# Experts by halves of the gate/up columns, token gather by fp32 matmuls for two experts at a time, a ring of 22 weight pieces

## The chip, the cores and the metric

One core of a Trainium2 chip runs one program. The metric is device time in microseconds (us) of one execution; lower is better.

## What is computed

One layer: a mixer of three branches over 256 tokens of width 1024, then a mixture of 32 experts of which each token takes 4, then a norm. All weights are fp32. The part that matters here is the expert stage and the few lines ahead of it:

```python
logits = (x @ w_router + b_router)                 # 256 tokens, 32 experts
top_logit, top_idx = lax.top_k(logits, 4)
top_w = jax.nn.softmax(top_logit, axis=-1)
...
xb = x[tok]                                        # the tokens of expert e
gu = xb @ w_gu[e] + b_gu[e]                        # 1024 x 2048
gate, up = jnp.split(gu, 2, axis=-1)
gate = jnp.minimum(gate, 7.0); up = jnp.clip(up, -7.0, 7.0)
act = (up + 1) * gate * jax.nn.sigmoid(1.702 * gate)
y[tok] += weight * (act @ w_down[e] + b_down[e])   # 1024 x 1024
...
out = rmsnorm(x + gate_ffn * y, norm_final)
```

## The kernel before, in words

The mixer and its projections take the first two fifths of the program. After them come the output projection (four column blocks `pr`, line 904 on), which builds the residual `x1` block by block and at once feeds the router matmuls (`lps`, line 933), then the router (lines 945 to 981), and then a loop over the 32 experts (line 1224).

An expert's weights are 12 pieces of 1 MiB, 128 rows of 8 KB: eight pieces of `w_gu`, one for each block of 128 input rows and with all 2048 gate and up columns, and four of `w_down`. `ew` (line 848) issues one DMA for a piece on the SP queue into the next tile of a ring. The ring has `NR = (8, 7, 4)`, 19 tiles, in three pools that are opened as the mixer's memory falls free. A load waits until the matmuls have read its tile's last piece, and the loads stand in one queue, so the ring decides how far the loads run ahead of the matmuls. The first loads are issued during the last mixer stages (`ew_ahead`).

At most 64 tokens are taken per expert. `gather` (lines 1005 to 1028) picks them by matmul with a one-hot matrix `oh`: `x1` times its row scale `rs2` is split into two fp32r parts `xshi` and `xslo` (lines 983 to 986, two on ACT and two on DVE of 128x1024), and four experts' tokens are gathered at once into `xe`, of which there are two buffers. An expert then runs

- `gate_up` (line 1046): for each of 8 row blocks `k` the gate tile `pg` and the up tile `pu`, each by two matmuls that fill partitions 0 to 63 and 64 to 127;
- `scatter` of the expert before (line 1087), the transposes for the way back (`swt_ps`), the bias matmul of the next expert's gate tile;
- `act_half` (line 1055) for columns of half `c`: min, sigmoid, products on DVE and ACT, transposes on PE (`act_ps`), copy on ACT; then `down_half`, four of eight row blocks of `w_down`; and both again for the second half.

The Tile framework's scheduler sets the order of the instructions on each engine and of the loads on SP from priorities (`issue_after` moves a block behind an instruction). At expert 29 `gain` (line 1107) broadcasts the final norm's gain by four matmuls on diagonal matrices that DVE builds. The last expert is finished by `down_finish` (line 1118): its down result in two column blocks of 256, the residual by matmuls with the identity (`ylast`), squares, root, and `norm` with the four output DMAs.

Each matmul of fp32 operands shows as two instructions in the trace, each transpose and each fp32r matmul as one.

Of the kernel before, what the change touches and what calls it, by code (L numbers as in the profile page):

```python
# [18 lines left out]
D = 1024  # L19
# [5 lines left out]
GRP = 4  # L25
# [55 lines left out]
def trace(tc, pools, I, out, dbg, stop):  # L81
# [746 lines left out]
    NR = (8, 7, 4)  # L828
    nload, lastew = [0], [None]

    DN_ORDER = (0, 1, 4, 5, 2, 3, 6, 7)
    gsrc = I["w_gu"].rearrange("e (q k p) n -> e q p k n", p=128, k=1)
    dsrc = I["w_down"].rearrange("e q p (k n) -> e q p k n", k=2)
# [14 lines left out]
    def ew(src):  # L848
        t = ew_tile()
        lastew[0] = SY.dma_start(t.rearrange("p (k n) -> p k n", k=src.shape[1]), src)  # L850
        return t

    epieces = iter([gsrc[e, q] if q < 8 else dsrc[e, DN_ORDER[2 * (q - 8)] // 2] for e in range(NE) for q in range(12)])
    ahead = []

    def ew_ahead(n):

        with tc.issue_after(last[0].ins):
            for _ in range(n):
                ahead.append(ew(next(epieces)))  # L860

    def ew_next():
        return ahead.pop(0) if ahead else ew(next(epieces))
# [5 lines left out]
    for br, (yhl, pw) in enumerate(((ybhl, "p_sb"), (yahl, "p_lru"), (None, "p_rwkv"))):  # L869
# [6 lines left out]
        for pr in range(4):  # L876
# [3 lines left out]
            if br == 2 and pr == KS:  # L880
                gmix = mt("gmix", [128, 512])
                row_bcast(adag[:, 0:4], gmix)
                keep_setup(mixer)
                bias_setup(mixer)
# [19 lines left out]
    for pr in range(4):  # L904
# [15 lines left out]
        if pr == 2:  # L920
            gmix = mt("gmix", [128, 512])
            row_bcast(adag[:, 4:8], gmix)
        for t in range(2):
            V.tensor_tensor(ps[:, t], ps[:, t], gmix[:, pr % 2 * 256:pr % 2 * 256 + 256], ALU.mult)
            V.tensor_tensor(x1[:, t, csl], x1[:, t, csl], ps[:, t], ALU.add)
            A.activation(ps[:, t], x1[:, t, csl], AF.Square, accum_out=sqp[:, t, pr:pr + 1])
# [4 lines left out]
            V.tensor_copy(xt, tp)  # L931
# [6 lines left out]
    pools.close(wsp, fin)  # L938
    moe2 = pools("moe2", bufs=1, side="right")
# [27 lines left out]
    for t in range(2):  # L967
        A.activation(wd[:, t], lg[:, t], AF.Exp, bias=sm[:, t, 0:1])
        A.activation(sm[:, t, 4:8], sm[:, t, 4:8], AF.Exp, bias=sm[:, t, 0:1], accum_out=sm[:, t, 1:2])
    V.reciprocal(sm[:, :, 1:2], sm[:, :, 1:2])  # L970
    for t in range(2):
        V.scalar_tensor_tensor(wd[:, t], wd[:, t], sm[:, t, 1:2], sel[:, t], ALU.mult, ALU.mult)
    dump("lg", lg)

    cps = ptp([128, NE], "cnt_ps")
    for t in range(2):
        T.matmul(cps[0:1], onesq[:, 0:1], sel[:, t], start=(t == 0), stop=(t == 1))
    cnt = mt("cnt", [1, 1])
    V.tensor_reduce(cnt, cps[0:1], AX.X, ALU.max)
    cnt_i = moe.tile([1, 1], I32, name="cnt_i")  # L980
    V.tensor_copy(cnt_i, cnt)

    xs = [mt2(n, [128, 2, D], dt=F32R) for n in ("xshi", "xslo")]
    for t in range(2):
# [20 lines left out]
    def gather_start(rks, n):  # L1005

        oh = mt2("oh", [128, 2, GRP, SLOTS], dt=F32R)
        for t in range(2):
            V.tensor_tensor(oh[:, t, 0:n], bcast(iot[:, 0:SLOTS], 1, n), bcast(rks[t], 2, SLOTS), ALU.is_equal)
        return oh, mt2("xe", [128, KT, GRP, SLOTS], 2)  # L1010

    def gather_part(oh, xe, n, ks):

        for k in ks:
            xps = ptp([128, 2, GRP, SLOTS], "xps")
            for kk in range(2):
                for t in range(2):
                    for i, x in enumerate(xs):
                        T.matmul(xps[:, kk, 0:n].rearrange("p e s -> p (e s)"), x[:, t, (k + kk) * 128:(k + kk + 1) * 128],  # L1019
                                 oh[:, t, 0:n].rearrange("p e s -> p (e s)"), start=(kk + t + i == 0), stop=(t + i == 2),  # L1020
                                 skip_group_check=True)
# [21 lines left out]
    def pgu_tile(name):  # L1043
        return psum.tile([128, 512], F32, name=name, tag="mm", bufs=3)

    def gate_up(pg, pu, gu, xe):
        for k in range(KT):
            for j, p in enumerate((pg, pu)):
                for hf in range(2):
                    c0 = j * D + hf * 512  # L1050
                    i = T.matmul(p[hf * 64:hf * 64 + 64], xe[:, k], gu[k][:, c0:c0 + 512], start=False, stop=(k == KT - 1),  # L1051
                                 skip_group_check=True)
        return i

    def act_half(c, pg, pu, ahead=False):

        csl = slice(c * 256, c * 256 + 256)
        g_, s_ = (mt2(n, [128, 256], b) for n, b in (("g_", 2), ("s_", 1)))
        V.tensor_scalar(g_, pg[:, csl], 7.0, None, ALU.min)
        A.activation(s_, g_, AF.Sigmoid, scale=1.702)  # L1060
        if ahead:
            sqrt_ahead(s_)
        V.tensor_tensor(g_, g_, s_, ALU.mult)
        V.tensor_scalar(s_, pu[:, csl], 7.0, -7.0, ALU.min, ALU.max)
        V.scalar_tensor_tensor(g_, s_, 1.0, g_, ALU.add, ALU.mult)
        tp = ptp([128, 2, 128], "act_ps")
# [5 lines left out]

    def down_half(pd, dn, c, at):
        for n in range(c * 4, c * 4 + 4):
            k = DN_ORDER[n]
            w = dn[n // 2][:, k % 2 * D:k % 2 * D + D]
            for hf in range(2):
                i = T.matmul(pd[hf * 64:hf * 64 + 64], at[:, k % 2, (k // 4) * 64:(k // 4) * 64 + 64],  # L1078
                             w[:, hf * 512:hf * 512 + 512], start=(n == 0), stop=(n == KT - 1))
# [7 lines left out]
    def scatter(yd, swt):  # L1087

        for t in range(2):
            for hf in range(2):  # L1090
# [4 lines left out]
                V.tensor_tensor(y[:, t, csl], y[:, t, csl], ps, ALU.add)  # L1095

    def expert(gu, dn, bias, xe, swt):
        pg, pu = pgu_tile("pg"), pgu_tile("pu")
        bias(0, pg)
        bias(1, pu)  # L1100
        gate_up(pg, pu, gu, xe)
        pd = pch([128, 512], "pd")
        for c in range(2):
            down_half(pd, dn, c, act_half(c, pg, pu))
        scatter(gated(pd), swt)

    def gain(t):

        for i in range(0, KT, 2):
            ps = pch([128, 256], "gfin")  # L1110
            T.matmul(ps, onesq, diag2(mt("gdiag", [128, 2, 128], 1, "s_w"), P("norm_final", i, 2)), start=True, stop=True)
            A.activation(t[:, i * 128:i * 128 + 256], ps, AF.Copy)
        return t

    PRE, LATE = 6, 4
    odst = out.rearrange("b (a p) d -> p (b a) d", p=128)

    def down_finish(ats, dn, swt, gfin):
# [3 lines left out]
        pds = [pch([128, 256], "pd") for _ in range(2)]  # L1122

        lastmm = [None]

        def down(n):
            k = DN_ORDER[n]
            w = dn[n // 2][:, k % 2 * D:k % 2 * D + D]
            for j in range(2):
                for hf in range(2):  # L1130
                    lastmm[0] = T.matmul(pds[j][hf * 64:hf * 64 + 64], ats[k % 4 // 2][:, k % 2, (k // 4) * 64:(k // 4) * 64 + 64],
                             w[:, hf * 512 + j * 256:hf * 512 + j * 256 + 256], start=(n == 0), stop=(n == KT - 1))

        for n in range(PRE):
            down(n)
        ys = [pmm("ylast") if i < 3 else pch([128, 512], "ylast") for i in range(4)]
        for i in range(4):
            with tc.issue_after(lastmm[0].ins) if i >= LATE else contextlib.nullcontext():
                T.matmul(ys[i], ident, y[:, i // 2, i % 2 * 512:i % 2 * 512 + 512], start=True, stop=False, skip_group_check=True)
# [197 lines left out]
```

## Time and profile before

| | us |
|---|---|
| runs shown: median of 3 | 1546.18 |
| lowest and highest of them | 1539.46, 1547.42 |
| the profiled execution, its own time | 1557.08 |
| its span (what the trace covers) | 1555.3 |
| PE busy in the span | 1458.0 (94%) |
| DVE, ACT, POOL busy | 638.5, 411.5, 11.0 |
| first and last expert load issued | 520.7, 1515.0 |
| mean granted TensorE clock | 0.969 of full |

Times inside the trace are counted from the span's start. Matmuls are pipelined and their ends are modelled: the pace of a row of matmuls is read from the starts, not from the length of one. "DMA" is the share of the 16 DMA engines that was busy. A granted clock of 1.00 is 2.4 GHz, of 0.50 is 1.2 GHz.

### The profile page before, as it was taken

To read this page: it belongs to the slowest core of one execution; us is meant where nothing else is said; L and a number is where in the kernel's file an instruction comes from. 1 tells how busy PE (TensorE), PEld (TensorE's weight loads), DVE (VectorE), ACT (ScalarE), POOL (GpSimd) and SP (SyncE) were. 2 spreads that over 40 slices of the span, in tenths; PEclk is the share of its full clock that TensorE was granted. 3 is DMA by queue.
4 is the path that set the end of the run, shared out by engine and by line. 5 is a ranking of instruction groups with operands and counts; after the bars stand their busy time and mean duration, and the time that the engine had idled before them with its cause. 6 is when DMAs were issued, how large, how long until landed. Compare 5 with 4: busy or idle time off the path is not lost. (4 is left out here: it accounts for less than half of the span.)

```text
span 1555.3 us, 21129 instructions
## 1 busy us (share of the span) xinstructions
PE 1458.0 (94%) x8592; PEld 834.1 (54%) x8592; DVE 638.5 (41%) x1322; ACT 411.5 (26%) x728; POOL 11.0 (1%) x59
## 2 busy tenths in 40 slices
PE   6999999999899998999999999999989989989897
PEld 4888989788899896333333333333223323323233
DVE  4677536689735664213223133123113113212313
ACT  4654335668534443001001001001001001001101
POOL 0000000000000000000000000000000000000000
PEclk8999889999899998999999999999999999999999
DMA  9455345346333876999999999999999999999994
GB/s 374 156 182 184 126 134 187 108 143 217 99 95 125 312 296 267 367 421 422 421 421 421 421 421 421 421 420 421 422 422 421 421 422 421 421 421 422 421 421 190
DMA packets 85686, 498.87 MB, mean 321 GB/s; under 512 B 12624, under 2 KB 12880, under 8 KB 36432
## 3 DMA queue, kind: packets, MB, share of 16 engines
q1 hardware_dynamic: 85584, 497.46, 80.4%
q8 instruction: 70, 1.15, 0.3%
q14 instruction: 32, 0.26, 0.0%
HBM read 496.37 MB, written 1.05 MB: 320 GB/s over the span
## 5 line engine op out<-in xcount | busy, mean ns | idle before, releaser
L1051 PE MATMUL pg<-ew,xe 128*64 128x512 f32 x1024 | 274.6, 600 | 20.5 <-DMA ew<-in_w_gu_dram 20.3
L1051 PE MATMUL pu<-ew,xe 128*64 128x512 f32 x1024 | 267.8, 593 | 0.0
L1078 PE MATMUL pd<-ew,act 128*64 128x512 f32 x992 | 233.0, 606 | 27.6 <-ACT act L1070 27.6
L168 PE MATMUL mm<-hhi,whi 128*128 128x256 f32 x656 | 193.2, 295 | 3.9 <-ACT gq L723 2.9
L168 PE MATMUL mm<-hhi,wlo 128*128 128x256 f32 x656 | 192.7, 294 | 3.4 <-DVE wlo L150 3.4
L168 PE MATMUL mm<-hlo,whi 128*128 128x256 f32 x656 | 191.3, 292 | 0.0
L150 DVE TENSOR_TENSOR wlo<-raw,whi 128x1024 fp32r<-128x1024 f32 x122 | 148.7, 1221 | 80.9 <-ACT whi L149 79.9
L1051 PEld LDWEIGHTS pg<-ew,xe 128*64 128x64 f32 x1024 | 70.6, 137 | 171.6 <-issue 103.6
L149 ACT ACTIVATE whi<-raw 128x1024 fp32r<-128x1024 f32 x122 | 128.6, 1057 | 123.1 <-PE mm L168 77.0
L1051 PEld LDWEIGHTS pu<-ew,xe 128*64 128x64 f32 x1024 | 76.4, 137 | 142.9 <-issue 140.4
L1078 PEld LDWEIGHTS pd<-ew,act 128*64 128x64 f32 x992 | 70.0, 138 | 153.9 <-issue 111.1
L168 PEld LDWEIGHTS mm<-hhi,whi 128*128 128x128 f32 x656 | 129.1, 197 | 12.3 <-issue 5.6
L168 PEld LDWEIGHTS mm<-hhi,wlo 128*128 128x128 f32 x656 | 128.9, 196 | 10.0 <-issue 5.1
L168 PEld LDWEIGHTS mm<-hlo,whi 128*128 128x128 f32 x656 | 129.1, 197 | 5.3 <-issue 4.8
L1084 DVE TENSOR_TENSOR yd<-pd,gff 128x512 f32<-128x512 f32 x31 | 21.5, 692 | 244.8 <-PE pd L1078 226.0
L1093 PE MATMUL pc<-yd,swt 64*128 64x512 f32 x248 | 96.0, 628 | 0.0
L1095 DVE TENSOR_TENSOR x<-x,pc 128x512 f32<-128x512 f32 x124 | 84.1, 681 | 9.3 <-PE pc L1093 8.3
L1093 PEld LDWEIGHTS pc<-yd,swt 64*128 64x128 f32 x248 | 30.0, 185 | 49.7 <-issue 29.9
L1023 ACT ACTIVATE xe<-xps,adaf,A 128x256 f32<-128x256 f32 x32 | 18.1, 564 | 96.2 <-DVE xe L1022 95.9
L1070 ACT ACTIVATE act<-act_ps 128x256 f32<-128x256 f32 x64 | 24.5, 383 | 59.9 <-PE act_ps L1068 58.8
L206 PE MATMUL adaps<-raw,crep 128*32 128x256 f32 x384 | 31.6, 433 | 7.9 <-DMA raw<-in_w_ada_dram 7.8
L1022 DVE TENSOR_SCALAR xe<-xps,A,adaf 128x256 f32<-128x256 f32 x32 | 17.4, 544 | 45.4 <-PE xps L1019 45.4
(814 smaller groups left out, 1769.2 us busy)
## 6 DMA issues: line engine op xcount, KB each, us to landing
ew<-in_w_gu_dram SPq DMA_DIRECT2D x256, 1024.0 KB, 19.8
ew<-in_w_down_dram SPq DMA_DIRECT2D x128, 1024.0 KB, 19.8
raw<-in_w_in_dram SPq DMA_DIRECT2D x90, 512.0 KB, 3.7
raw<-in_w_ada_dram SPq DMA_DIRECT2D x48, 512.0 KB, 4.5
raw<-in_p_sb_dram SPq DMA_DIRECT2D x8, 512.0 KB, 4.1
raw<-in_p_lru_dram SPq DMA_DIRECT2D x8, 512.0 KB, 3.4
raw<-in_p_rwkv_dram SPq DMA_DIRECT2D x8, 512.0 KB, 7.5
raw<-in_w_out_dram SPq DMA_DIRECT2D x8, 512.0 KB, 4.6
```

Source lines behind the costliest of these rows:

```text
L149: A.activation(hi, src, AF.Copy)
L150: V.tensor_tensor(lo, src, r32(hi), ALU.subtract)
L168: T.matmul(ps[:, c], w[i][:, k, c * 128:c * 128 + 128], x[j][:, q * 4 + k], start=(q + c + k + n == 0), stop=(q == 1 and k == 3 and n == 2 ...
L206: T.matmul(ps[32 * j:32 * j + 32], crep[:, q * 4 + j, :], raw[q][:, j], start=(q == 0), stop=(q == 1))
L1022: V.tensor_scalar(xe[:, k, 0:n], xps[:, 0, 0:n], A2[:, k:k + 1], sh2[:, k:k + 1], ALU.mult, ALU.add)
L1023: A.activation(xe[:, k + 1, 0:n], xps[:, 1, 0:n], AF.Identity, scale=A2[:, k + 1:k + 2], bias=sh2[:, k + 1:k + 2])
L1051: i = T.matmul(p[hf * 64:hf * 64 + 64], xe[:, k], gu[k][:, c0:c0 + 512], start=False, stop=(k == KT - 1), skip_group_check=True)
L1070: A.activation(at, tp, AF.Copy)
L1078: i = T.matmul(pd[hf * 64:hf * 64 + 64], at[:, k % 2, (k // 4) * 64:(k // 4) * 64 + 64], w[:, hf * 512:hf * 512 + 512], start=(n == 0), st ...
L1084: V.tensor_tensor(yd, pd, gff2, ALU.mult)
L1093: T.matmul(ps, swt[sl, t], yd[sl], start=True, stop=True)
L1095: V.tensor_tensor(y[:, t, csl], y[:, t, csl], ps, ALU.add)
```

## The change

- `w_gu` is laid out on the host as eight pieces of another cut: four pieces for gate and up columns of half 0 (each 256 + 256 columns of either partition half, two row blocks), then four for half 1. `gate_up` runs one half into one PSUM tile `pgu`; its activations (`act_chain`) follow at once, and the transposes (`act_back`) stand behind the other half's matmuls. The biases are laid out to match.
- The split into `xshi` and `xslo` goes. `oh` holds `rs2` at the hits instead of 1, and the gather multiplies fp32 `x1` by it: for two experts (`GRP = 2`) at a time, so 16 times in place of 8, into one `xe` buffer. `y` becomes a tile of its own, since `x1` stays in use.
- A fourth ring pool of 3 tiles is opened where `wsp` and `fin` close, so the ring has 22 tiles. `gmix` moves into `wsp`.
- In the output projection the squares go to a PSUM tile of their own, and the copies `x1t` go from DVE to ACT. The softmax weights and the count (`weights`) are traced behind the first one-hots.
- `gain` becomes one DMA that broadcasts `norm_final` into a ring tile, issued behind the last expert's loads.
- Last expert: the last piece is loaded as two halves; `w_down` pieces are cut so that column quarters `j` lie together; the second down blocks run for `j = 0`, then `j = 1`, each followed by its gating, scatter, squares and product with the gain; `end_norm` scales.

```diff
-GRP = 4
+GRP = 2
-    NR = (8, 7, 4)
+    NR = (8, 7, 4, 3)
...
-    epieces = iter([gsrc[e, q] if q < 8 else dsrc[e, DN_ORDER[2 * (q - 8)] // 2] for e in range(NE) for q in range(12)])
+    epieces = iter([(gsrc[e, q] if q < 8 else dsrc[e, q - 8], 2 if e == NE - 1 and q == 11 else 1)
+                    for e in range(NE) for q in range(12)])
...
-            A.activation(ps[:, t], x1[:, t, csl], AF.Square, accum_out=sqp[:, t, pr:pr + 1])
+            A.activation(pch([128, 256], "sqj"), x1[:, t, csl], AF.Square, accum_out=sqp[:, t, pr:pr + 1])
...
-            V.tensor_copy(xt, tp)
+            A.activation(xt, tp, AF.Copy)
...
     pools.close(wsp, fin)
+    ring_open()
+    ew_ahead(NR[3])
...
-    xs = [mt2(n, [128, 2, D], dt=F32R) for n in ("xshi", "xslo")]
-    for t in range(2):
-        A.activation(xs[0][:, t], x1[:, t], AF.Copy, scale=rs2[:, t:t + 1])
-        V.scalar_tensor_tensor(xs[1][:, t], x1[:, t], rs2[:, t:t + 1], r32(xs[0][:, t]), ALU.mult, ALU.subtract)
-    y = x1
+    y = mt2("y", [128, 2, D])
...
-        oh = mt2("oh", [128, 2, GRP, SLOTS], dt=F32R)
-        for t in range(2):
-            V.tensor_tensor(oh[:, t, 0:n], bcast(iot[:, 0:SLOTS], 1, n), bcast(rks[t], 2, SLOTS), ALU.is_equal)
-        return oh, mt2("xe", [128, KT, GRP, SLOTS], 2)
+        oh = mt2("oh", [128, 2, GRP, SLOTS])
+        for e in range(n):
+            for t in range(2):
+                V.tensor_scalar(oh[:, t, e], iot[:, 0:SLOTS], rks[t][:, e:e + 1], rs2[:, t:t + 1], ALU.is_equal, ALU.mult)
+        return oh, mt2("xe", [128, KT, GRP, SLOTS])
...
-                    for i, x in enumerate(xs):
-                        T.matmul(xps[:, kk, 0:n].rearrange("p e s -> p (e s)"), x[:, t, (k + kk) * 128:(k + kk + 1) * 128],
+                    T.matmul(xps[:, kk, 0:n].rearrange("p e s -> p (e s)"), x1[:, t, (k + kk) * 128:(k + kk + 1) * 128],
...
+    def gate_up(p, c, gu, xe, ks=range(KT)):
+        for k in ks:
+            w = gu[c * 4 + k // 2].rearrange("p (k h n) -> p k h n", k=2, h=2)[:, k % 2]
+            for hf in range(2):
+                i = T.matmul(p[hf * 64:hf * 64 + 64], xe[:, k], w[:, hf], start=False, stop=(k == KT - 1),
+                             skip_group_check=True)
...
+        for j in range(2):
+            js = slice(j * 256, j * 256 + 256)
+            for n in (6, 7):
+                for hf in range(2):
+                    down_mm(pds[j], dn, n, at, hf, slice(j, j + 1))
             V.tensor_tensor(yd[:, js], pds[j], gff2[:, js], ALU.mult)
...
+                    A.activation(ptp([128, 256], "junk"), p, AF.Square, accum_out=ss[:, t, j * 2 + hf:j * 2 + hf + 1])
+                    V.tensor_tensor(o_[:, t, n:n + 256], p, gfin[:, n:n + 256], ALU.mult)
...
-    xe, swt = gather(*ranks_of(0)), back_of(0)
+    oh, xe = gather_start(*ranks_of(0))
+    weights()
+    gather_part(oh, xe, GRP, range(0, KT, 2))
...
-        i = gate_up(pg, pu, gu, xe[:, :, e % GRP])
+        i = gate_up(p0, 0, gu, x)
+        g0 = act_chain(p0)
         with tc.issue_after(i.ins):
             if held:
-                scatter(*held)
+                scatter(*held, first=(e == 1))
...
+            i = gate_up(p1, 1, gu, x)
...
+        g1 = act_chain(p1, end)
+        with tc.issue_after(i.ins):
+            at = act_back(g0)
```

Where it moves instructions. DVE in the router, before: `lg` are the scaled logits, `m_6530` the four greatest, `sel` the chosen experts, `rk` a token's place in its expert.

```order
L956 MEMSET m_6530 128x2x4
L986 SCALAR_TENSOR_TENSOR xslo<-x_4491,rs_6522,xshi 128x1024
L958 MATCH_REPLACE sel<-m_6530,lg 128x32 x2
L986 SCALAR_TENSOR_TENSOR xslo<-x_4491,rs_6522,xshi 128x1024
L959 TENSOR_TENSOR sel<-sel,lg 128x64
```

The same place now:

```order
L960 MEMSET m_6547 128x2x4
L962 MATCH_REPLACE sel<-m_6547,lg 128x32 x2
L963 TENSOR_TENSOR sel<-sel,lg 128x64
L977 RECIPROCAL sm<-sm 128x2
L979 SCALAR_TENSOR_TENSOR wd<-wd,sm,sel 128x32 x2
L970 TENSOR_TENSOR rk<-tp,sel 128x32
```

The two `xslo` stood between the logits and `sel`; nothing stands there now.

PE in an expert late in the loop (from the matmuls of its first pieces to its last down matmul), before; the `pg` and `pu` pair stands eight times in all ahead of these rows:

```order
L1093 MATMUL pc<-yd,swt 128x512 x3
L1037 MATMUL swt_ps<-ident,s_w 128x128 x2
L1213 MATMUL pg<-bgt,pick 128x512
L1093 MATMUL pc<-yd,swt 128x512
L1068 MATMUL act_ps<-ident,g__9432 128x128 x2
L1078 MATMUL pd<-ew,act 64x512 x8
```

The same stretch now, of an expert behind which a gather stands:

```order
L1055 MATMUL pgu<-ew,xe 64x512 x16
L1103 MATMUL pc<-yd,swt 128x512 x3
L1055 MATMUL pgu<-ew,xe 64x512 x4
L1103 MATMUL pc<-yd,swt 128x512
L1055 MATMUL pgu<-ew,xe 64x512 x12
L1075 MATMUL act_ps<-ident,g__10745 128x128 x2
L1041 MATMUL swt_ps<-ident,s_w 128x128 x2
L1210 MATMUL pgu<-bgt,pick 128x512
L1083 MATMUL pd<-ew,act 64x512 x8
L1023 MATMUL xps<-oh,x_4491 128x128 x8
```

The scatter stands inside the second half's matmuls, and the first half's transposes stand directly behind them.

PE at the first expert, now. `ew_5158` and `ew_5286` are the first and second piece of half 0, `ew_5692` the first piece of half 1.

```order
L1055 MATMUL pgu_6625<-ew_5158,xe_6573 64x512 x2
L1055 MATMUL pgu_6627<-ew_5692,xe_6573 64x512 x2
L1023 MATMUL xps_6601<-oh_6568,x1_4491 128x128 x4
L1055 MATMUL pgu_6625<-ew_5158,xe_6573 64x512 x2
L1055 MATMUL pgu_6627<-ew_5692,xe_6573 64x512
L1055 MATMUL pgu_6625<-ew_5286,xe_6573 64x512
L1023 MATMUL xps_6608<-oh_6568,x1_4491 128x128 x4
L1055 MATMUL pgu_6625<-ew_5286,xe_6573 64x512 x3
```

Here both halves run side by side between groups of four gather matmuls; eight gather matmuls stand ahead of these rows. The first piece falls free behind the fourth row, the second behind the last.

## Rows read from the trace of the kernel before

**Rows 1.** The page, part 2: GB/s moved in 40 equal slices of the span.
```profile
GB/s 374 156 182 184 126 134 187 108 143 217 99 95 125 312 296 267 367 421 422 421 421 421 421 421 421 421 420 421 422 422 421 421 422 421 421 421 422 421 421 190
```

**Rows 2.** The page, part 6: issues of a line, KB each, median us to landing.
```profile
ew<-in_w_gu_dram SPq DMA_DIRECT2D x256, 1024.0 KB, 19.8
```

**Rows 3.** Windows: length, busy per engine (count), then PE clock, DMA share, GB/s.
```profile
600.00:605.00 5.00, 1.05 (x7) 0.97 (x7) 4.10 (x17) 4.53 (x9) 0.00 (x0) 0.63 0.37 156
605.00:610.00 5.00, 4.90 (x26) 4.46 (x28) 2.47 (x11) 0.56 (x1) 0.00 (x0) 0.50 0.01 3
610.00:615.00 5.00, 5.00 (x22) 2.08 (x24) 1.09 (x2) 1.13 (x2) 0.00 (x0) 0.85 0.23 66
...
635.00:640.00 5.00, 5.00 (x22) 2.23 (x20) 0.85 (x2) 0.80 (x2) 0.00 (x0) 1.00 0.35 146
```

**Rows 4.** Timeline of the SP queue: start, length, issue, count.
```profile
574.97 12.75 SPq L850 DMA_DIRECT2D ew<-in_w_gu_dram  x7
...
612.67 0.33 SPq L850 DMA_DIRECT2D ew<-in_w_gu_dram  x1
...
639.34 5.38 SPq L850 DMA_DIRECT2D ew<-in_w_gu_dram  x5
```

**Rows 5.** Timeline of the router: start, length, engine, line, operation.
```profile
601.30 1.27 DVE L986 SCALAR_TENSOR_TENSOR xslo<-x,rs,xshi 128x1024 fp32r<-128x1024 f32 x1
...
602.81 1.28 DVE L986 SCALAR_TENSOR_TENSOR xslo<-x,rs,xshi 128x1024 fp32r<-128x1024 f32 x1
...
604.00 0.22 DVE L959 TENSOR_TENSOR sel<-sel,lg 128x64 f32<-128x64 f32 x1
...
606.23 0.55 PE L1019 MATMUL xps<-oh,xshi 128*128 128x256 f32 x1
...
609.91 1.86 PE L1051 MATMUL pg<-ew,xe 128*64 128x512 f32 x4
```

**Rows 6.** Timeline of PE, an expert that waits for no load.
```profile
1184.71 1.08 PE L1051 MATMUL pg<-ew,xe 128*64 128x512 f32 x4
...
1198.60 1.98 PE L1093 MATMUL pc<-yd,swt 64*128 64x512 f32 x6
...
1202.16 0.44 PE L1068 MATMUL act_ps<-ident,g__9432 128*128 128x128 f32 x2
1203.14 3.66 PE L1078 MATMUL pd<-ew,act 128*64 128x512 f32 x16 [0.53 <-ACT act L1070]
...
1207.97 3.65 PE L1078 MATMUL pd<-ew,act 128*64 128x512 f32 x16 [0.53 <-ACT act L1070]
1211.46 1.03 PE L1051 MATMUL pg<-ew,xe 128*64 128x512 f32 x4
```

**Rows 7.** Timeline of PE: half a gather, first and last; fp32 matmuls of 128 columns.
```profile
1182.60 0.39 PE L1019 MATMUL xps<-oh,xshi 128*128 128x256 f32 x1
...
1184.50 0.28 PE L1019 MATMUL xps<-oh,xslo 128*128 128x256 f32 x1
...
190.79 1.16 PE L533 MATMUL nps<-sav,bk 128*128 128x128 f32 x8
```

**Rows 8.** Timeline of PE: a wait for a load, in brackets, late in the loop.
```profile
1222.49 1.08 PE L1051 MATMUL pg<-ew,xe 128*64 128x512 f32 x4 [0.54 <-DMA ew<-in_w_gu_dram]
```

**Rows 9.** Timeline of PE and a window, around the broadcast of the norm's gain.
```profile
1478.78 5.19 PE L1078 MATMUL pd<-ew,act 128*64 128x512 f32 x16 [0.32 <-ACT act L1070]
...
1472.00:1476.00 4.00, 2.73 (x5) 1.32 (x6) 0.94 (x3) 0.77 (x2) 0.00 (x0) 0.50 1.01 420
```

**Rows 10.** A window and the timeline of PE at the end of the program.
```profile
1530.00:1535.00 5.00, 5.00 (x19) 2.24 (x20) 3.31 (x8) 2.67 (x5) 0.00 (x0) 1.00 0.39 164
...
1527.28 1.03 PE L1051 MATMUL pu<-ew,xe 128*64 128x512 f32 x4
...
1534.41 5.40 PE L1131 MATMUL pd<-ew,act 128*64 128x256 f32 x48
...
1540.79 1.95 PE L1131 MATMUL pd<-ew,act 128*64 128x256 f32 x16
```

More of the change, by code (lines that the diff above doesn't have):

```diff
@@ L859, in ew_ahead @@
             for _ in range(n):
-                ahead.append(ew(next(epieces)))
+                ahead.append(ew(*next(epieces)))
     def ew_next():
-        return ahead.pop(0) if ahead else ew(next(epieces))
+        return ahead.pop(0) if ahead else ew(*next(epieces))
     mhl, KS = None, 1
@@ L1094, in scatter @@
                 csl = slice(hf * 512, hf * 512 + 512)
-                V.tensor_tensor(y[:, t, csl], y[:, t, csl], ps, ALU.add)
+                V.tensor_tensor(y[:, t, csl], (x1 if first else y)[:, t, csl], ps, ALU.add)
     def expert(gu, dn, bias, xe, swt):
[L1098 to L1101, printed above, removed]
+        ats = []
+        for c in range(2):
+            p = pgu_tile()
+            bias(c, p)
+            gate_up(p, c, gu, xe)
+            ats.append(act_back(act_chain(p)))
@@ L1102, in expert, with gain @@
         pd = pch([128, 512], "pd")
         for c in range(2):
-            down_half(pd, dn, c, act_half(c, pg, pu))
+            down_half(pd, dn, c, ats[c])
         scatter(gated(pd), swt)
[L1107 to L1112, printed above, removed]
+    def gain():
+        t = ew_tile()[:, 0:D]
+        SY.dma_start(t, I["norm_final"][0].partition_broadcast(128))
@@ L1120, in down_finish @@
+    def down_finish(pds, dn, at, swt, gfin):
         o_ = ew_tile().rearrange("p (t d) -> p t d", t=2)
         ss = mt("ss2", [128, 2, 8], 1, "m8")
[L1122 to L1128, printed above, removed]
+        for n in (4, 5):
             for j in range(2):
                 for hf in range(2):
-                    lastmm[0] = T.matmul(pds[j][hf * 64:hf * 64 + 64], ats[k % 4 // 2][:, k % 2, (k // 4) * 64:(k // 4) * 64 + 64],
-                             w[:, hf * 512 + j * 256:hf * 512 + j * 256 + 256], start=(n == 0), stop=(n == KT - 1))
@@ L1134, in down_finish @@
[L1134 to L1139, printed above, removed]
-        for n in range(PRE, KT):
-            down(n)
+                    i = down_mm(pds[j], dn, n, at, hf, slice(j, j + 1))
@@ L1144, in down_finish @@
             js = slice(j * 256, j * 256 + 256)
+            for n in (6, 7):
+                for hf in range(2):
+                    down_mm(pds[j], dn, n, at, hf, slice(j, j + 1))
             V.tensor_tensor(yd[:, js], pds[j], gff2[:, js], ALU.mult)
@@ L1284, in trace @@
             gu = [ew(gsrc[bass.ds(e, 1), q][0]) for q in range(8)]
[L1285 removed]
+            dn = [ew(dsrc[bass.ds(e, 1), q][0]) for q in range(4)]
             for b in range(1, S // SLOTS):
```

194 lines of the change are left out of this document (103 added, 91 removed).

## Prediction

> **What bounds the kernel now.** I read the page's bandwidth line first, then windows of five us where that line changes, then the SP queue and PE around the gaps. The line sits at 421 GB/s from the eighteenth slice to the last but one [rows 1]: the expert stage moves weights as fast as they come. A piece of 1 MiB takes 1.048576 MB / 421 GB/s = 2.49 us, the twelve of an expert 29.9 us. A load lands 19.8 us after its issue [rows 2], eight pieces of 2.49, so the queue is eight deep and the matmuls wait for it, not it for them: late in the loop PE stops half a us for a piece [rows 8], while an expert that waits for nothing takes 1211.46 - 1184.71 = 26.75 us [rows 6].
>
> So two things set the end. One is **when the queue runs without a gap**. The loads fill 19 tiles and stop near 602: the DMA share falls from 0.37 to 0.01 [rows 3], and the next load is issued at 612.67, when the first expert's first piece has been read [rows 4]. A second hole stands before 640 (0.35): the 28th load waits until 639.34. From there the loads run through. The other is **what comes after the last landing**. The engines fall quiet at 1530 + 0.39 x 5 = 1531.95 [rows 10], the span ends at 1555.3, 23.35 us later. In that tail PE is behind: it reads the last piece until 1540.79 + 1.95 = 1542.74, 10.8 us after it landed. Part of that lag was made earlier: building the norm's gain stalled PE and the granted clock was 0.50, 1.2 GHz, in 1472 to 1476, where sixteen down instructions took 5.19 us for 3.65 at full clock [rows 6, 9].
>
> **The first gap.** The router's chain runs on DVE: `sel` at 604.00, first gather matmul at 606.23, first expert matmul at 609.91 [rows 5]. Both `xslo` (1.27 and 1.28 us) stood ahead of `sel` and go: `sel` at 601.45. The `x1t` copies leave DVE too, and the square no longer holds the PSUM tile that DVE multiplies; I take 0.8 us for both, so 600.6. Against it, the softmax weights now stand ahead of `rk` on DVE; I take 0.6 us (below 0.4, above 1.5, the table load and exponents of ACT late by that much). First gather matmul: 600.6 + 2.23 + 0.6 = 603.4.
>
> An fp32 matmul of 128 columns is two instructions; eight such instructions took 1.16 us, of which the last one's modelled end is some 0.3: 0.112 each [rows 7]. The sixteen ahead of the first expert take 1.8 us at full clock, 3.6 at half, which is what this place had (0.50, [rows 3]). The first expert matmul then stands at 605.2 to 607.0; I take 606. The bounds are 604.8, and 609.9 if nothing of this is on the path.
>
> A matmul of `gate_up` costs 13.89 / 32 = 0.434 us [rows 6], a detour of four gather matmuls 0.9 + 0.3. By the new order the first piece is free after six matmuls and one detour, 3.8 us, the second after eight more steps' worth (two matmuls, a detour, three matmuls), 3.4 us: 606 + 7.2 + 0.5 for a clock still low = 613.7. Meanwhile the three new tiles keep the DMA busy 7.5 us longer, to about 609.4; their pool opens when the last output-projection products are read, before 599, so I cost that wait at nothing. What follows, in the order of the releases, is one piece per 1.7 us at most times, faster than 2.49, and the hole before 640 closes: the load that now needs the first down piece is the 35th, not the 28th.
>
> So: before, 27 pieces had landed at 639.34 + 0.8 (from issue to flow) = 640.1. After, 23 have landed at 613.7 + 0.8 = 614.5. The last landing moves by 640.1 - 614.5 - 4 x 2.49 = **15.6 us** earlier. With the bounds of the first matmul it is 10.5 to 17.
>
> **The loop.** PE's own time per expert changes, and DMA covers it as long as it stays under 29.9. The wait of 0.98 us from `act_ps` to the first down matmul [rows 6] is now filled by `swt_ps` and the bias matmul that stood elsewhere: 26.75 - 0.75 = 26.0. The gather: half of one took 1184.50 - 1182.60 + 0.2 = 2.1 us for four experts [rows 7], so about 4.2 us per four. Now 32 instructions per two experts, 32 x 0.112 = 3.6 us plus switches and waits for PSUM, 4.4: 2.2 us per expert instead of 1.05. Together **28.2 us**, 1.7 under DMA. I cost it at nothing, but its cover is thin. At 640 the queue would be 23 + 25.5 / 2.49 = 33 pieces on, PE about 17, so PE has some 37 us to make up, and about 8 for the expert that adds the down biases, in 29 experts at 1.7, 49 us. It arrives with about 4 us to spare. Moving four activations of a half behind matmuls, DVE's 64-column one-hots and the smaller evacuations are off the path: DVE is busy 41% of the span.
>
> **The tail**, counted from the last landing. The last gate/up piece lands 4 x 2.49 = 9.95 us before it; four matmuls, 1.7, end at -8.2. One identity matmul 0.9, transposes and copy 1.0, the first down piece 1.8 (sixteen instructions at 5.40 / 48 = 0.112, [rows 10]), two identity matmuls 1.7, transposes 1.0, two pieces 3.6, one identity matmul 0.9, the last piece 1.8: +4.4 instead of +10.8, **6.4 us**. The lag that the norm's gain made is gone with it: that becomes one DMA behind the last weights. From the last down matmul to the end were 12.6 us; gating, squares and products of the first columns now run beside the second's, for which I take 1.0. Tail: **7.4 us**, between 0 if PE is late and 9.
>
> **The sum.** 15.6 + 7.4 = 23.0 us off the profiled execution, 1557.08 to 1534.1. That execution stood 10.9 us above the median of the runs shown, which itself lies in a spread of 8 us. Off the median: 1546.18 - 23.0 = **1523**.
>
> **Rivals.**
> - **PE does not catch up.** If an expert costs PE 28.6 instead of 28.2, the 4 us to spare become 29 x 0.4 - 4 = 8 late at the last expert, and the tail's gain is gone: 1531. For it: the cover is thin and PSUM tiles for the gather are shared with the transposes. Against it: the early experts' order leaves PE fewer gaps than the stretch of rows 6. 0.20.
> - **The three tiles fill late.** If the new pool waits for something past 609, 7.5 us go: 1531. Against it: nothing in its releasers runs that late. 0.06.
> - **Slower: the fp32 gather makes PE the bound.** Place: the 32 instructions between two experts. At 0.224 us each, the half-clock price, a pair's gather costs 8 us, an expert 30, PE never catches up, and ends some 48 us behind: 1571. It decides from 0.17 us per instruction, where an expert is 29.1 us and the lag eats all 23. Against it: 0.112 [rows 7]. 0.06.
> - **The clock falls in the waits.** When PE has caught up it waits 1.7 us per expert. In this trace waits of 0.54 us stand between matmuls at the full-clock 0.27 us each [rows 8], and the long one beside the gain stands with 0.50 [rows 9]. Should each of the last seven experts lose its clock for 11 us, each would lose 5.5 - 1.7 = 3.8 us, 27 in all: 1550. [...] 0.03.
>
> **Chances and range.** Forecast 0.63, rivals as given, 0.02 for the rest. A measurement of this kernel can tell some 0.5%, 7.7 us, from no change. Faster by more holds the forecast and nearly all of the first two rivals, 0.88; within it 0.05; slower 0.07. The forecast's own bounds are 16 to 26 us, 1520 to 1530; with the spread of the runs, 4 us to either side, and the first rival, 1513 to 1537.
>
> **What would show it.** Right: no xslo; `sel` near 601 and the first expert matmul near 606; the DMA share without a hole after 615 and none before 609; last landing 13 to 17 us earlier in the span; PE waits for loads again in the last experts; under 19 us from the last landing to the end. Wrong: gather instructions further apart than 0.15 us, an expert above 28.5 us, no waits for loads at the end, a granted clock under 1.00 late in the loop, or a hole in the DMA share near 640.

## Result and the profile after

Ten executions of the change took 1528.99 to 1540.28 us, median **1534.23**; ten of the kernel before 1539.46 to 1555.27, median 1546.80. The ratio is 0.992, 95% interval 0.9903 to 0.9937: 12.6 us faster, about 10 to 15. Forecast were 23 us and 1523, range 1513 to 1537. The sign, the side of 0.5% and the range hold; the size came out at little more than half. Two of the timed executions of the experiments below (1912.0 us in the kernel with the earlier way back, 1802.0 in the one with two stalls) ran at mean granted clocks of 0.73 and 0.74 and are left out of every median and ratio.

The page's bandwidth row, as [rows 1], reaches the ceiling one slice earlier, in the seventeenth instead of the eighteenth:

```profile
GB/s 378 159 183 184 163 153 170 110 166 182 91 97 120 279 301 371 423 420 422 421 421 421 421 422 421 421 421 421 421 421 421 421 421 421 422 420 421 421 421 229
```

The windows that answer to [rows 3] (length, busy per engine, then PE clock, DMA share, GB/s):

```profile
600.00:605.00 5.00, 5.00 (x29) 3.50 (x28) 0.82 (x2) 0.92 (x2) 0.00 (x0) 0.83 1.02 419
605.00:610.00 5.00, 5.00 (x24) 2.21 (x25) 1.34 (x5) 0.92 (x2) 0.00 (x0) 1.00 0.60 203
610.00:615.00 5.00, 5.00 (x24) 1.60 (x23) 0.97 (x4) 1.67 (x2) 0.00 (x0) 1.00 0.68 246
...
635.00:640.00 5.00, 5.00 (x26) 1.71 (x24) 0.00 (x0) 0.00 (x0) 0.00 (x0) 1.00 1.02 423
```

The stretch with shares of 0.01 and 0.23 now shows 0.60 and 0.68, and the hole before 640 is gone. SP's queue shows why: load after load is issued as pieces are read, from 606.27 on, where before nothing was issued until 612.67 [rows 4]. Two views of it, the wide one and a window:

```profile
570.90 22.47 SPq L851 DMA_DIRECT2D ew<-in_w_gu_dram  x8
593.41 17.84 SPq L851 DMA_DIRECT2D ew<-in_w_down_dram  x4
611.78 13.45 SPq L851 DMA_DIRECT2D ew<-in_w_gu_dram  x8
...
606.27 0.33 SPq L851 DMA_DIRECT2D ew<-in_w_down_dram  x1
```

The router's timeline, as [rows 5]; no `xslo` stands on DVE, and PE waits 1.83 us for `sel` where it waited 3.95:

```profile
596.60 0.23 DVE L963 TENSOR_TENSOR sel<-sel,lg 128x64 f32<-128x64 f32 x1
...
598.88 3.38 PE L1023 MATMUL xps<-oh,x 128*128 128x128 f32 x16 [0.65 <-DVE rk L970]
602.20 1.94 PE L1055 MATMUL pgu<-ew,xe 128*64 128x512 f32 x8
```

PE in the middle of the loop, as [rows 6, 7], an expert that is followed by a gather and the next one that isn't. From 1059.35 to 1085.79 is 26.44 us without a gather:

```profile
1046.88 3.65 PE L1083 MATMUL pd<-ew,act 128*64 128x512 f32 x16
1050.46 2.05 PE L1023 MATMUL xps<-oh,x 128*128 128x128 f32 x16
...
1057.37 2.05 PE L1023 MATMUL xps<-oh,x 128*128 128x128 f32 x16
1059.35 7.09 PE L1055 MATMUL pgu<-ew,xe 128*64 128x512 f32 x32
...
1085.79 7.04 PE L1055 MATMUL pgu<-ew,xe 128*64 128x512 f32 x32
```

The first wait for a load comes at 1372, as [rows 8]:

```profile
1369.53 1.94 PE L1055 MATMUL pgu<-ew,xe 128*64 128x512 f32 x8
1372.01 1.94 PE L1055 MATMUL pgu<-ew,xe 128*64 128x512 f32 x8 [0.55 <-DMA ew<-in_w_gu_dram]
```

The stretch that held the norm's gain, as [rows 9], at full clock:

```profile
1450.00:1500.00 50.00, 47.08 (x217) 16.82 (x213) 11.15 (x24) 4.41 (x12) 0.00 (x0) 1.00 1.01 421
```

The end, as [rows 10], first in windows, then PE's last down matmuls:

```profile
1510.00:1515.00 5.00, 4.58 (x28) 2.44 (x30) 1.28 (x3) 2.55 (x5) 0.00 (x0) 1.00 0.69 283
1515.00:1520.00 5.00, 5.00 (x40) 2.70 (x38) 0.00 (x0) 0.00 (x0) 0.00 (x0) 1.00 0.18 70
```

```profile
1514.44 3.67 PE L1083 MATMUL pd<-ew,act 128*64 128x256 f32 x32
...
1519.10 1.95 PE L1083 MATMUL pd<-ew,act 128*64 128x256 f32 x16
```

**One ruler for all profiles.** The two profiled executions differ by 21.0 us (1557.08 and 1536.04), the medians by 12.6. So I measured each profile from one mark that lies ahead of every part of the change: PE's transposes of the router's weights, `tp<-wr`. Three profiles of before and three of the change (the first two rows and the experiments below):

| kernel, profile | mark at | first expert matmul | moved in 180 us | last packet of the loads | last down matmul ends | end |
|---|---|---|---|---|---|---|
| before, first | 527.76 | +82.15 | 62.85 MB | +1006.9 | +1014.98 | +1027.54 |
| the change, first | 523.73 | +78.47 | 69.28 MB | +993.1 | +997.32 | +1010.57 |
| before, again | 515.81 | +82.15 | 63.16 MB | +1006.7 | +1014.56 | +1027.19 |
| before, a third | 523.83 | +81.90 | 62.80 MB | +1007.0 | +1016.00 | +1028.57 |
| the change, again | 525.25 | +78.69 | 68.85 MB | +994.3 | +998.44 | +1011.65 |
| the change, a third | 516.85 | +78.87 | 68.53 MB | +994.3 | +998.45 | +1011.25 |

The megabytes are summed over 36 windows of five us from the mark; "last packet" is where, in the trace, the last DMA packet of the weights and of the norm's gain ends. In the first profile of before that is 1534.66, in that of the change 1516.86; the windows of one us on either side of it, before and now (the 16 GB/s in the last row are one packet of the queue that fetches instructions):

```profile
1533.66:1534.66 1.00, 1.00 (x6) 0.47 (x6) 0.11 (x1) 0.15 (x1) 0.00 (x0) 1.00 0.10 41
1534.66:1535.66 1.00, 1.00 (x12) 0.70 (x10) 0.00 (x0) 0.24 (x1) 0.00 (x0) 1.00 0.00 0
```

```profile
1515.86:1516.86 1.00, 1.00 (x12) 0.64 (x10) 0.00 (x0) 0.00 (x0) 0.00 (x0) 1.00 0.39 156
1516.86:1517.86 1.00, 1.00 (x12) 0.57 (x8) 0.00 (x0) 0.00 (x0) 0.00 (x0) 1.00 0.07 16
```

In this ruler the kernels repeat within 1.4 us, and **from the mark on the change is worth 16.6 us** (1027.8 to 1011.2). The mark itself stands anywhere from 516 to 528.

### The profile page after: what moved, and what is told of

Its sections match the earlier page's. It is cut to its first block, busy times and chain, and to the rows that moved or that the text cites. A ratio compares the mean times of both kernels' runs of the same rounds, so it can differ in the third digit from the quotient of the medians.

```text
span 1534.3 us, 21738 instructions
## 1 busy us (share of the span) xinstructions
PE 1472.5 (96%) x8840; PEld 846.6 (55%) x8840; DVE 659.3 (43%) x1392; ACT 415.9 (27%) x774; POOL 11.0 (1%) x59
## 4 chain that ended last, share of the span: by engine, by line
PE 74%; DMA 19%; DVE 3%; ACT 2%; issue 1%; SPq 0%; ACTq 0%; DVEq 0%
PE pgu L1055 21%; PE mm L170 19%; DMA ew<-in_w_gu_dram 13%; PE pd L1083 10%; DMA ew<-in_w_down_dram 5%; PE pc L1103 4%; PE xps L1023 3%; PE adaps L208 2%; PE mm L915 2%; PE z L519 1%; PE mm L182 1%; DVE wlo L152 1%; PE act_ps L1075 1%; PE gps L455 1%; ACT act L1077 1%
## 5 line engine op out<-in xcount | busy, mean ns | idle before, releaser
L1055 PE MATMUL pgu<-ew,xe 128*64 128x512 f32 x2048 | 472.8, 597 | 5.3 <-DMA ew<-in_w_gu_dram 5.3
L1055 PEld LDWEIGHTS pgu<-ew,xe 128*64 128x64 f32 x2048 | 140.5, 136 | 298.1 <-issue 269.8
L1083 PE MATMUL pd<-ew,act 128*64 128x512 f32 (+1 forms) x1056 | 239.0, 585 | 14.9 <-ACT act L1077 13.3
L1105 DVE TENSOR_TENSOR y<-y,pc 128x512 f32<-128x512 f32 x120 | 81.5, 683 | 49.5 <-PE pc L1103 49.2
L1027 ACT ACTIVATE xe<-xps,adaf,A 128x128 f32<-128x128 f32 x64 | 29.3, 457 | 181.3 <-DVE xe L1026 181.3
L1023 PEld LDWEIGHTS xps<-oh,x 128*128 128x128 f32 x512 | 61.0, 195 | 26.7 <-issue 25.2
L1023 PE MATMUL xps<-oh,x 128*128 128x128 f32 x512 | 67.3, 285 | 0.7 <-DVE rk L970 0.7
L1026 DVE TENSOR_SCALAR xe<-xps,A,adaf 128x128 f32<-128x128 f32 x64 | 26.2, 410 | 75.0 <-PE xps L1023 75.0
```

What stands on the lines that cost most here:

```text
L1023: T.matmul(xps[:, kk, 0:n].rearrange("p e s -> p (e s)"), x1[:, t, (k + kk) * 128:(k + kk + 1) * 128], oh[:, t, 0:n].rearrange("p e s -> p ...
L1027: A.activation(xe[:, k + 1, 0:n], xps[:, 1, 0:n], AF.Identity, scale=A2[:, k + 1:k + 2], bias=sh2[:, k + 1:k + 2])
L1055: i = T.matmul(p[hf * 64:hf * 64 + 64], xe[:, k], w[:, hf], start=False, stop=(k == KT - 1), skip_group_check=True)
L1083: return T.matmul(dst[hf * 64:hf * 64 + 64].rearrange("p (j n) -> p j n", n=256), at[:, k % 2, (k // 4) * 64:(k // 4) * 64 + 64], w, start ...
L1105: V.tensor_tensor(y[:, t, csl], (x1 if first else y)[:, t, csl], ps, ALU.add)
```

## Experiments

**The kernel before, twice more** (no edit).

> The kernel before, unchanged. Its profiled execution took 1557.08 us, 10.3 over the median of ten (1546.80); that of the change took 1536.04, 1.8 over its own (1534.23). The two profiles so differ by 21.0, the medians by 12.6. Theory one: the profiled execution of before lost some 10 us by its granted clock (mean 0.969), about 4 ahead of the output projection and the rest around the first gather, which ran at 0.50; then a second profile of it, near 1547, has a higher mean clock, the two transposes of the router's weights near 524 instead of 527.8, and its first expert matmul 6 to 10 us earlier than 609.9, with about the same 945 us from there to the end. Rival: the start is as it was (609 to 611) and the expert stage itself is shorter (935 to 938 us from the first expert matmul to the end).

> The kernel before once more, for a third profile of it. Theory one: mean clock, first expert matmul and end go together as in the run before this one, and from the first expert matmul to the end it is 943 to 947 us. Rival: that stretch differs by over 4 us between the profiles.

They took 1544.78 and 1554.12 us at mean clocks of 0.978 and 0.969. Theory one holds in the main: from the mark to the end 1027.2 and 1028.6, and from the first expert matmul to the end 945.0 and 946.7 us against 945.4. One part of it is wrong: what sets the profiles apart lies ahead of the mark and not around the first gather, since the first expert matmul stands as late behind the mark in all three (81.9 to 82.2). Four rows of the third profile follow; its windows ahead of the mark show nearly the same granted clocks as the change's first (0.83, 0.74, 0.86, 0.76 and 0.83, 0.74, 0.85, 0.76 in four windows of 20 us from 360 on), and the marks stand 0.1 apart:

```profile
523.83 1.87 PE L787 MATMUL tp<-wr,adaf 128*128 128x32 f32 x16
...
600.43 1.03 PE L963 MATMUL tp<-sel,before 128*128 128x32 f32 x4 [3.95 <-DVE sel L959]
602.29 0.55 PE L1019 MATMUL xps<-oh,xshi 128*128 128x256 f32 x1
605.73 1.08 PE L1051 MATMUL pg<-ew,xe 128*64 128x512 f32 x4
```

The change, from the same mark:

```profile
523.73 1.87 PE L789 MATMUL tp<-wr,adaf 128*128 128x32 f32 x16
...
596.97 0.60 PE L967 MATMUL tp<-sel,before 128*128 128x32 f32 x4 [1.83 <-DVE sel L963]
```

With equal clocks ahead the spans are 1552.4 and 1534.3, 18 us apart. So 4 of the 7.7 us by which the first expert matmul stands earlier in the first two profiles (609.91 and 602.20) are not the change's.

**The change, twice more and timed** (no edit).

> The changed kernel, unchanged, for a second profile of it. From the transposes of the router's weights to the end it was 1027.5, 1027.2 and 1028.6 us in three profiles of the kernel before, and 1010.6 in the one of the change: 17 less, where the medians differ by 12.6. Theory one: that stretch is 1010 to 1012 us again, and what the medians hide is chance in the clock of the stages ahead, which the change leaves alone (the transposes stand at 516 to 528). Rival: the stretch itself varies more than before, by 3 to 6 us, because PE has no time to spare in it, so that an execution whose clock falls there ends later; then a window of it shows a granted clock under 1.00 or a first expert matmul late against the transposes.

> The changed kernel once more, for a third profile. Theory one: 1010 to 1012 us from the transposes of the router's weights to the end. Rival: over 1013.

> The changed kernel again, timed, since three profiles of each show 16.6 us less from the transposes of the router's weights to the end (1027.8 to 1011.2), and the ten medians only 12.6. Theory one (the rest is chance in the clock ahead of that place): ratio 0.988 to 0.991. Rival (the executions of the change do lose about 4 us more ahead of that place, though the same instructions stand there): ratio 0.991 to 0.993.

The two profiles give 1011.65 and 1011.25: theory one. A fourth, of the timed run, gives 1010.8. But twelve executions had a median of 1534.15, ratio 0.9918 (0.9893 to 0.9943): the rival's ratio, though the interval reaches into theory one's. More executions tell them apart. The mark of an execution without a profile can be reckoned from its time, less 1.74 us outside the span and less the kernel's own 1027.8 or 1011.1. For 61 executions of before it is 517.6 on average, for the 22 timed of the change 521.8 (uncertain by 0.6 and 0.9). By this reckoning about 4 of the 16.6 us are given back ahead of the mark, in stages whose instructions are the same. The granted clocks on record agree: an execution's span times the share of the clock that it lacked is 36.7 us on average over 62 executions of before and 32.0 over the 22 of the change; the profiles lose 16.2 and 6.1 of that behind the mark, which leaves 20.5 and 25.9 ahead of it. Seen in a trace it is not: the marks of the seven profiles average 522.5 before and 521.3 now, too few at a scatter of 12 us.

**A ring of 19.**

```diff
-    NR = (8, 7, 4, 3)
+    NR = (8, 7, 4)
...
-    ring_open()
-    ew_ahead(NR[3])
     moe2 = pools("moe2", bufs=1, side="right")
```

> The changed kernel with 19 pieces in the ring instead of 22; all else as changed. Theory one (the end is set by when the weights run without a gap): three pieces fewer fit ahead of the first expert, 3 x 2.49 = 7.5 us later, ratio to before about 0.997; the gap in the DMA share near 600 grows to some 12 us. Rival one (the router and the order of the early experts made the gain, and the tiles were filled late anyway): within 2 us of the change, ratio 0.992. Rival two (with 19 tiles the later pieces wait for the first down piece again): 10 to 13 us later than the change, ratio 0.999 to 1.001.

Ratio 0.9972 (0.9947 to 0.9997), from the mark to the end 1018.7: 7.6 us more than the change, 7.5 expected. The gap, with the mark at 524.97:

```profile
600.00:605.00 5.00, 4.87 (x20) 4.02 (x22) 1.77 (x8) 0.91 (x2) 0.00 (x0) 0.50 0.02 7
605.00:610.00 5.00, 5.00 (x22) 1.86 (x18) 0.41 (x1) 0.46 (x1) 0.00 (x0) 0.99 0.08 13
610.00:615.00 5.00, 5.00 (x25) 2.31 (x26) 1.89 (x7) 0.97 (x3) 0.00 (x0) 1.00 0.61 223
```

The three tiles are filled in time, and each is worth one piece. No second hole followed (a DMA share of 1.01 in each window of five us from 620 to 640), so the hole near 640 closes without the three tiles; that it is the order of the early experts that closes it is the prediction's account and was not tested by itself.

**The router's chain put back.**

```diff
-            A.activation(pch([128, 256], "sqj"), x1[:, t, csl], AF.Square, accum_out=sqp[:, t, pr:pr + 1])
+            A.activation(ps[:, t], x1[:, t, csl], AF.Square, accum_out=sqp[:, t, pr:pr + 1])
...
-            A.activation(xt, tp, AF.Copy)
+            V.tensor_copy(xt, tp)
...
     V.tensor_scalar(sm[:, :, 0:1], m8[:, :, 0:1], -1.0, None, ALU.mult)
+    for t in range(2):
+        V.scalar_tensor_tensor(y[:, t], x1[:, t], rs2[:, t:t + 1], x1[:, t], ALU.mult, ALU.subtract)
     V.tensor_copy(sm[:, :, 4:8], m8[:, :, 0:4])
```

> The changed kernel with three things of the router put back: DVE copies the transposed tokens, the square is written into the tile that DVE multiplies, and two products of 128x1024 stand on DVE ahead of the router's selection (they write y, which the first expert's result overwrites). Theory one (that chain is on the path, and the weights wait for the first expert): first expert matmul 3 to 4.5 us later against the same execution's transposes of the router's weights, and the end later by as much, ratio 0.994 to 0.995. Rival (the pieces already in the ring cover it): the first expert matmul is later but the last landing is not, ratio 0.992.

From the mark the first expert matmul is at +82.0 (3.3 later) and the end at +1015.2 (4.1 later), with 67.21 MB moved, 1.6 MB or 3.8 us less than the change: the chain is on the path, as theory one has it. Its ratio, 0.9925 (0.9897 to 0.9954), stands at the rival's 0.992, and its interval holds both; by the reckoning above its six executions reached the mark near 517. Without the ruler this run would have decided nothing, or the wrong thing.

**The gather twice, and left out.** The first edit repeats the loop's gather matmuls; the second, `more = False`, leaves them out, so that every later expert works on the tokens of the first two.

```diff
-            for kk in range(2):
+            for kk in [0, 1] * again:
...
-                gather_part(oh, xe1, GRP, (0, 2))
+                gather_part(oh, xe1, GRP, (0, 2), 2)
```

> The changed kernel with every matmul of the gathers inside the loop issued twice (the second one writes the same sums again), 16 more matmuls, 32 instructions, per two experts. Theory one (an expert costs PE about 28.2 us, DMA 29.9, and the cover is thin): 32 x 0.112 = 3.6 us per pair, 1.8 per expert, 30.0 us: PE just becomes the bound, its early lag of some 35 us is never made up, no wait for a load is seen at the end, and the end comes 25 to 40 us later than the change, ratio 1.008 to 1.018. Rival (PE has more room than I thought, since the order of the early experts leaves fewer gaps): under 10 us later, ratio under 0.999, with waits for loads in the last experts.

> The changed kernel without the gathers inside the loop: every expert after the second works on the tokens of the first two, so that the fifteen other gathers and their one-hots are left out. Theory one (the gather is hidden behind the weights, and the tail after the last landing is set by the last expert alone): within 2 us of the change, ratio 0.991 to 0.993; PE waits for loads from about 900 on instead of 1210. Rival (the chain of PE through the first half of the loop holds the weights back): 3 to 8 us faster than the change, ratio 0.987 to 0.990.

Twice: 1579.16, ratio 1.0198 (1.0159 to 1.0237), 44 us more than the change from the mark (1055.4). A pair of experts takes 59.99 us, 30.0 each, as expected, and PE waits for no load; the price is a little over my range.

```profile
1034.52 7.09 PE L1055 MATMUL pgu<-ew,xe 128*64 128x512 f32 x32
...
1094.51 7.09 PE L1055 MATMUL pgu<-ew,xe 128*64 128x512 f32 x32
```

Left out: ratio 0.9922 (0.9895 to 0.9949) and 1011.1 us from the mark, the change's own number, while PE waits 43.5 us for gate/up pieces instead of 5.3 (the waits of the page after 640, per releaser in us, times, longest):

```profile
PE pgu L1055 <- DMA ew<-in_w_gu_dram: 43.5, 77, 1.8
```

So the gather is free at its price, and not at twice its price.

**The ending.** First the last piece whole and the kernel before's ending; then, in a kernel of its own, the way back of the last expert but one moved forward.

```diff
-    epieces = iter([(gsrc[e, q] if q < 8 else dsrc[e, q - 8], 2 if e == NE - 1 and q == 11 else 1)
+    epieces = iter([(gsrc[e, q] if q < 8 else dsrc[e, q - 8], 1)
...
+        square(0, 0)
+        square(0, 1)
+        square(1, 0)
+        total(0)
...
```

```diff
+        if end:
+            i = gate_up(p0, 0, gu, x, range(0, 4))
+            with tc.issue_after(i.ins):
+                i = scatter(*held)
+            with tc.issue_after(i.ins):
+                i = gate_up(p0, 0, gu, x, range(4, 8))
```

> The changed kernel with its last piece loaded whole and with the ending of the kernel before: gating after the last down matmul, then the products with the way back, four squares of 512 columns, and the norm's scale and gain in one instruction of DVE. My prediction's term (the first columns' gating, squares and products run beside the second's, 1.0 us, and the half piece saves 0.6): from the last down matmul to the end 14 us and the last down matmul 0.6 later, 1.6 us slower than the change. Rival, from the profile of the change (eight squares of 256 columns hold ACT for 3.3 us where four of 512 took 2.5, and the second columns' products wait 0.58 for DVE to have read the first): from the last down matmul to the end 12.4 to 12.8 instead of 13.1, within 0.7 us of the change either way. Both lie near what five rounds can tell; the profile decides.

> The ending of the run before this one, and in the last expert the eight products of the way back of the expert before it stand after the second piece of its gate/up columns instead of after the fourth, where PE waits 0.54 us for each piece. Theory one (the lag of PE behind the last landing, 3.9 us, is work of the last expert that the weights don't cover): the waits in front of the third and fourth piece are filled, the last down matmul comes 1.0 to 1.6 us earlier after the DMA goes quiet, and the end as much earlier than in the run before this one. Rival (the order of DVE and the PSUM tiles set it): no change in that distance, below 0.4.

The old ending took 12.8 us from the last down matmul to the end, the change's own 11.9 to 13.3 in four profiles, before's 12.6; ratio 0.990 (0.9864 to 0.9935), 1011.9 from the mark. The rival holds: ending by quarters gains nothing that the profiles show. The halved last piece doesn't either: the last down matmul ends 4.2 us behind the last packet with the piece whole and 4.1 to 4.2 in the change, where the text on record had 0.6 between them. Where a part of the overlap goes, PE's rows of the change's second profile show: the products for the second columns wait until DVE has read the first ones.

```profile
1523.62 1.13 PE L1167 MATMUL ylast<-yd,swt 64*128 64x256 f32 x8
1525.34 1.86 PE L1167 MATMUL ylast<-yd,swt 64*128 64x256 f32 x8 [0.58 <-DVE ew L1172]
```

The second kernel kept the change's ending; the text on record says the ending of the run before it, which is wrong. Its last down matmul ends 3.2 us behind the last packet, against 4.1 to 4.2 in the change: 1.0 us, as theory one has it. From the mark it ends at 1010.6 (the change: 1010.6 to 1011.7), and the timed result (0.9917, 0.9884 to 0.995) can't show one us. PE's waits in front of the third and fourth piece are gone:

```profile
1489.87 1.94 PE L1055 MATMUL pgu<-ew,xe 128*64 128x512 f32 x8 [0.55 <-DMA ew<-in_w_gu_dram]
1491.73 3.02 PE L1103 MATMUL pc<-yd,swt 64*128 64x512 f32 x8
1494.69 7.09 PE L1055 MATMUL pgu<-ew,xe 128*64 128x512 f32 x32
```

Neither version is shown to beat the change.

**Two stalls**, in the kernel without the loop's gathers.

```diff
+        for _ in range(hold):
+            V.tensor_scalar(g_, g_, 1.0, None, ALU.mult)
...
-        g1 = act_chain(p1, end)
+        g1 = act_chain(p1, end, 32 if e in (16, 24) else 0)
```

> The kernel without the gathers inside the loop (every expert after the second works on the tokens of the first two), and in it 32 more products by one on DVE in the chain of the seventeenth and the twenty-fifth expert, 13.4 us each, of which PE should stand still for about 10. PE waited 50 us for loads in that kernel, so both stalls are covered, and from the transposes of the router's weights to the end it should be 1011 us again. What is asked: sixty-one executions of the kernel before stand, by their times less 1027.8, at 517.6 on average at those transposes, sixty-three of the change and its variants at 521.2, though the instructions ahead are the same. Theory one (clock that is not lost in the expert stage, where the kernel before lost 10 us of full-speed time at no cost, is lost ahead of it): with two stalls in which the clock falls the mean clock stays at 0.979 and the median falls by 3 to 5 us, to 1529 to 1531. Rival (the clock ahead has nothing to do with it): the mean clock falls to 0.974 to 0.976 and the median stays at 1533 to 1536.

In both stalls PE stood 5.09 us instead of 10, and by the trace for a load: matmuls of the next expert stand ahead of the stalled ones. The clock fell all the same, and the eight matmuls behind it took 3.68 us for 1.94. It fell a third time, at an expert without a stall, where PE had stood 2.24 us for a piece of `w_down`. The row of the first stall and this one, and the three windows:

```profile
1067.04 3.68 PE L1055 MATMUL pgu<-ew,xe 128*64 128x512 f32 x8 [5.09 <-DMA ew<-in_w_gu_dram]
...
1361.74 2.99 PE L1085 MATMUL pd<-ew,act 128*64 128x512 f32 x8 [2.24 <-DMA ew<-in_w_down_dram]
```

```profile
1050.00:1100.00 50.00, 44.21 (x182) 14.01 (x182) 20.26 (x56) 3.70 (x11) 0.00 (x0) 0.93 1.01 421
1300.00:1350.00 50.00, 44.30 (x185) 13.97 (x181) 19.87 (x53) 3.15 (x9) 0.00 (x0) 0.93 1.01 422
1350.00:1400.00 50.00, 45.00 (x188) 14.14 (x186) 11.16 (x25) 3.60 (x11) 0.00 (x0) 0.97 1.01 421
```

Five executions took 1528.92 to 1534.13, median 1533.07, mean 1532.2, at mean clocks of 0.974 to 0.978, 0.976 on average. The clock is the rival's; the time lies between the two, and five executions (ratio 0.9905, 0.9873 to 0.9937, which is some 1526 to 1536 us) can't part them. So that the clock lost in the loop comes back ahead of it is not shown, nor is it ruled out, and why executions of the change should stand 4 us later at the mark stays open.

## Why the prediction was right, and where its size was off

By its own steps, on the ruler (averages of three profiles of before and four of the change):

- **What bounds the kernel.** Right: weights at 421 GB/s, and the end set by when they run without a gap and by what follows the last of them. Leaving the loop's fifteen gathers out changed nothing; three tiles fewer cost three pieces.
- **The first gap.** Forecast 3.9 us for the first expert matmul (609.9 to 606), measured 3.4 (82.07 to 78.73). By its parts: the products with `sel` start 3.4 earlier (76.6 to 73.2 from the mark), as forecast; from there to the first gather matmul it is 1.9 us in both, so that the softmax weights cost nothing where I took 0.6; and the sixteen gather instructions took 3.3 to 3.7 us, near the half-clock bound of 3.6, where I took 2.6.
- **The flow of weights.** Forecast 15.6 us earlier, measured 14.0: 68.82 MB in 180 us from the mark against 62.94, 5.88 MB at 421 GB/s. Of the 1.6 us short, 0.5 is the first expert matmul; the rest was not traced. The hole near 640 closed as forecast.
- **The loop.** Forecast 28.2 us of PE per expert, measured 28.36 (1085.96 to 1142.66 is 56.7 for a pair, by the chain of waits). The catch-up, 4 us to spare, came at 1372, four experts before the end at 1.5 each: 6 us to spare. Both clear; costed at nothing, and nothing it cost.
- **The tail: here the sum failed.** I put 7.4 us, 6.4 of it in "+4.4 instead of +10.8" and 1.0 for the overlap of the quarters. Measured from the last packet the last down matmul ends at +4.2 (4.1 to 4.2) instead of +8.3 (7.8 to 9.0). So the +4.4 was right, and the mis-sized term is the +10.8: its zero, "1530 + 0.39 x 5 = 1531.95", treats the DMA as busy in full until it stops, while it thins out to about 0.63 of its engines for six us and the last packet ends at 1534.66. The change thins out much as before, so that this is not the difference between the two kernels; but the zero put 2.7 us of the loads' own time into PE's lag. The 6.4 us were 4.2. A second term was not in the sum at all: of the 14.0 us of the flow 12.7 arrive at the last packet, and the norm's gain, 0.52 MB or 1.25 us at 421 GB/s, which now lands with the last weights, accounts for the rest. The overlap of the quarters was worth nothing (12.6 us from the last down matmul to the end before, 12.8 now). From the flow to the end the tail so gained 2.7 us, not 7.4.
- **The sum.** 14.0 - 1.3 + 4.2 - 0.2 = 16.7, measured 16.6, where I had 23.0.
- **What no step had.** By the reckoning from the times 4 us more are lost ahead of the mark: a measured 12.6 of 16.6. I subtracted from a median as if that part stood still. It is about the 4 us that I gave the runs' spread, but it goes one way.
- **What was luck.** The measured 1534.23 lies outside the forecast's own bounds of 1520 to 1530. It is inside the range by the 4 us for the spread and by the room for the first rival, PE not catching up, which did not happen.

The rivals: PE did catch up; the tiles were filled in time; PE did not become the bound, though the doubled gather showed that rival's place and price (30.0 us per expert, 44 us; I had 48); and the clock did not fall in the waits. On that last one, the trace keeps the granted clock at 1.00 from 1350 to 1500 with eleven waits of half a us, and in the kernel without gathers (1.00 in every window of 50 us from 650 to 1500) with 77 waits of up to 1.8. It fell to 0.50 behind the two waits of 5.09 and beside the one of 2.24, and in the kernel with the doubled gather beside a wait of 1.52 us for DVE (0.97 in the window from 950 to 1000), so that the length of a wait alone doesn't tell. The Trainium skill, "TensorE: Matmul & The Clock Gate", section "Loop structure matters more than you think", shows as its bad case a loop with a long wait for a DMA ahead of every matmul, 8 us in its drawing. No wait in these loops was as long, and the rival's loop, with waits of half a us, is not that one.

## What to carry to other kernels

Measure a stage from a mark ahead of everything that the edit touches: here it took the scatter from 16 us down to 1.4 and turned a ratio that decided nothing into an answer. It doesn't see what moves ahead of the mark, so the whole time is needed beside it. Where a stream of loads sets the end, count three things apart: when it starts to flow, when its last packet lands, and what the engines still owe after that; a zero worked out from a volume books the loads' own last microseconds as slack of the engines. A prefetch ring was worth one transfer per tile here, since the tiles were filled while the engines were busy with something else.

## What the runs showed that I had not expected

- The same instructions ahead of the mark take 516 to 528 us, mostly by their granted clock: the mark less the time lost by the clock is 493 to 498 in all fourteen profiles of before, the change and its variants, and the loss 19 to 32.
- The change gets rid of stretches at half clock inside the loop (0.93 in 950 to 1000 and 0.90 in 1450 to 1500 before, 1.00 in both now), and still, by its times, reaches the mark some 4 us later on average. Whether stalls put into the loop undo that, five executions couldn't tell.
- The DMA thins out to about 0.63 of its engines for the last six us of the weights in every profile but that of the doubled gather, where PE was the bound. By an estimate from these shares (0.37 of six us) that is some two us that a volume count doesn't see.
